# Strassen's seven block products for the FFNs' down projections, placed between the steps of the next group

## The chip, the cores and the metric

The kernel runs on one core of a Trainium2 chip. The metric is the device time of one execution in microseconds (us), the median of several. The core's engines are TensorE (PE in the profile: matrix multiplication; PEld is its weight load), VectorE (DVE), ScalarE (ACT), GpSimd (POOL) and SyncE (SP), which here issues the DMAs. Each works through its own queue in order; semaphores tie them together.

## What is computed

Two layers of a diffusion backbone: 512 latent tokens and 256 context tokens of width 1024. Each layer has four attention mixers and a feed-forward network (FFN) with a depthwise convolution over the tokens; layer 1 needs the latent tokens alone. What the change touches is the FFN:

```
def conv_ffn(h, w_up, conv_w, conv_b, w_down):
    u = depthwise_conv(h @ w_up, conv_w, conv_b)
    a, v = u[..., :FFN_DIM], u[..., FFN_DIM:]
    return (jax.nn.silu(a) * v) @ w_down

x = x + mod[:, 5, None] * rms_norm(f, g_ffn_post[l])
```

FFN_DIM is 2816, so w_up is 1024 x 5632 and w_down is 2816 x 1024. All is float32.

## The kernel before

Float32 products are made from halves. split (L249 on ACT, L255 on DVE or POOL) copies a value to a rounded "hi" in the type fp32r and takes the rest as "lo"; a product is then three matmuls, hi hi, hi lo and lo hi (mm3 at L268 to L270, token_mm at L1132). On POOL, split works in steps of 256 columns. Weights come by a DMA on SP (L260, 512 KB each) into the tile wr and are split into wh and wl.

The FFN is ffn_main, once a layer. FFN_DIM is cut into 22 blocks of 128. For a block there are two "ups" (the a half and the v half): 8 x 3 matmuls of 512 latent tokens and, in layer 0, 8 x 3 of 258 columns for the context, into a PSUM tile "up" (two of them). Each is followed by the convolution: ACT at L1226, DVE at L1227 and L1229, into the tile ut. Behind both stand Silu (ACT, L1233), the multiplication (DVE, L1234), the split of the result into gh and gl (POOL), and the load and split of the block's 1024 columns of w_down.

Blocks are taken in groups of [3, 3, 4, 4, 4, 4]. Behind a group, each token tile (128 tokens: six in layer 0, four in layer 1) gets its down projection from the group's blocks: per block three passes of two 512-column matmuls, six in all, with the tokens stationary, into a PSUM tile "dn" (two of them). It is copied to the accumulator of that tile by ACT (first group, L1267) or added by DVE (L1269). Behind the last group, post_norm normalises each token tile (Square on ACT at L550, a reciprocal square root in nine small DVE steps at L287 to L297, DVE at L587, the residual at L588 on POOL, on DVE for the last tile) and the tile is stored.

In layer 0, three steps of mod_steps stand at the end of each block: they multiply rows of the modulation weights (DMA into the tile wm, six buffers) by the conditioning vector on DVE (L502), once for each of one or two vectors.

The program doesn't run in the order in which it is written. The framework orders every engine's queue beforehand along a modelled time, by readiness and then by program order, and that order is then fixed; so a group's down matmuls stand in part between the ups of the same group and in part between those of the next.

## Time and profile before

| | us |
|---|---|
| median of 3 executions | 1946.42 |
| lowest and highest | 1942.38, 1950.67 |
| the profiled execution | 1949.91 |
| its span, first to last instruction | 1947.8 |
| mean granted clock of TensorE | 0.962 of full speed |

The span has layer 0's mixers up to about 540 us, its FFN to about 1120, layer 1's mixers to about 1475, its output projection to about 1575, and its FFN to the end. Times in rows are microseconds from the span's start unless marked ns. A row of a timeline gives start, length, engine, line, operation, out<-in and a count, and in brackets the idle time before it with what ended it. The end of a matmul is modelled, and matmuls overlap: a difference of starts is what one occupies.

### The profile page before, as it was taken

How to read it: one execution, taken by the hardware profiler on the slowest of the kernel's cores; microseconds unless marked ns; L12 is line 12 of the kernel's file. 1: busy time of each engine (PE TensorE's matmuls, PEld its weight loads, DVE VectorE, ACT ScalarE, POOL GpSimd, SP SyncE). 2: the span in 40 equal slices, each digit the busy share in tenths (PEclk: the TensorE clock that was granted, in tenths of full speed). 3: DMA queues.
4: the chain of work that ended last, by engine and by line, in shares of the span. 5: the costliest groups of instructions: out<-in, count | busy, mean ns of one | idle time of the engine just before them, and what ended most of it. 6: DMA issues, size and time to landing. Idle time of an engine off the chain costs nothing.

```text
span 1947.8 us, 27218 instructions
## 1 busy us (share of the span) xinstructions
PE 1809.6 (93%) x9834; PEld 1534.7 (79%) x9834; DVE 1085.1 (56%) x2119; ACT 905.4 (46%) x1597; POOL 995.0 (51%) x1216
## 2 busy tenths in 40 slices
PE   6999999898988999999999978979899899999997
PEld 3878788776887878888888867768787788888885
DVE  5456777775769545354322665775875622333335
ACT  4546557885542323131323454654886444333332
POOL 1464544544258547263625445753555265656653
PEclk7999899999998999999999999989999879999999
DMA  8663352644355324241312136524253322323322
GB/s 317 174 195 120 111 175 88 177 111 153 110 186 182 113 93 174 82 178 70 126 33 92 61 128 149 146 74 107 83 156 109 109 90 93 99 87 97 109 87 86
DMA packets 76166, 240.02 MB, mean 123 GB/s; under 512 B 11136, under 2 KB 12672, under 8 KB 73216
## 3 DMA queue, kind: packets, MB, share of 16 engines
q1 hardware_dynamic: 76032, 238.28, 38.8%
q8 instruction: 78, 1.28, 0.3%
q14 instruction: 56, 0.46, 0.1%
HBM read 201.94 MB, written 36.31 MB: 122 GB/s over the span
## 4 chain that ended last, share of the span: by engine, by line
PE 54%; DVE 7%; ACT 3%; issue 2%; POOL 2%; DMA 1%; SPq 0%; ACTq 0%; POOLq 0%; DVEq 0%
PE dn L1132 14%; PE up L268 9%; PE up L270 9%; PE up L269 9%; PE s L825 2%; PE wo L1132 2%; PE po L901 1%; PE tp L894 1%; DVE rs_w L293 1%; PE pj L268 1%; PE pj L269 1%; PE pj L270 1%; DVE rs_y L297 1%; DVE ptl L255 1%; DVE acc L587 1%
## 5 line engine op out<-in xcount | busy, mean ns | idle before, releaser
L255 POOL TENSOR_TENSOR wl<-wr,wh 128x256 fp32r<-128x256 f32 x706 | 568.4, 840 | 399.2 <-ACT wh L249 379.3
L249 ACT ACTIVATE wh<-wr 128x1024 fp32r<-128x1024 f32 (+1 forms) x186 | 193.6, 1050 | 401.6 <-PE up L269 202.7
L1227 DVE SCALAR_TENSOR_TENSOR ut<-up,pc,ut 128x769 f32<-128x769 f32 (+1 forms) x84 | 74.1, 883 | 347.5 <-ACT ut L1226 343.6
L268 PE MATMUL up<-hx,wh 128*128 128x512 f32 x672 | 263.2, 392 | 0.0
L269 PE MATMUL up<-hx,wh 128*128 128x512 f32 x672 | 262.6, 391 | 0.0
L270 PE MATMUL up<-hx,wl 128*128 128x512 f32 x672 | 262.4, 391 | 0.0
L825 PE MATMUL s<-op 128*128 128x256 f32 (+4 forms) x648 | 156.9, 351 | 21.4 <-ACT P L842 12.2
L255 DVE TENSOR_TENSOR ptl<-tp,pth 128x512 fp32r<-128x512 f32 (+1 forms) x208 | 136.1, 663 | 37.0 <-ACT pth L249 35.6
L870 POOL TENSOR_SCALAR P<-P,st 128x768 f32<-128x768 f32 (+2 forms) x120 | 96.7, 807 | 105.6 <-DVE st L846 70.4
L270 PEld LDWEIGHTS up<-hx,wl 128*128 128x128 f32 x672 | 126.5, 188 | 27.3
L268 PEld LDWEIGHTS up<-hx,wh 128*128 128x128 f32 x672 | 126.6, 188 | 25.5
L269 PEld LDWEIGHTS up<-hx,wh 128*128 128x128 f32 x672 | 126.6, 188 | 25.2
L1132 PE MATMUL dn<-wh,gh 128*128 128x512 f32 x440 | 140.4, 400 | 5.4 <-ACT gh L249 5.4
L1132 PE MATMUL dn<-wh,gl 128*128 128x512 f32 x440 | 137.5, 400 | 5.3 <-POOL gl L255 5.3
L825 PEld LDWEIGHTS s<-op 128*128 128x128 f32 (+1 forms) x648 | 108.7, 194 | 42.4 <-ACT P L842 20.7
L1132 PE MATMUL dn<-wl,gh 128*128 128x512 f32 x440 | 140.3, 398 | 0.0
L894 PE MATMUL tp<-ident,P 128*128 128x128 f32 x800 | 128.3, 282 | 10.0 <-DVE ptl L255 4.6
L255 POOL TENSOR_TENSOR gl<-ut,gh 128x256 fp32r<-128x256 f32 (+1 forms) x132 | 91.7, 722 | 75.9 <-ACT gh L249 74.1
L249 ACT ACTIVATE pth<-tp 128x512 fp32r<-128x512 f32 (+1 forms) x208 | 116.9, 577 | 29.1 <-PE tp L894 27.9
L842 ACT ACTIVATE P<-s,st 128x768 f32<-128x768 f32 (+2 forms) x120 | 94.3, 787 | 62.4 <-DVE st L833 25.2
L901 PE MATMUL po<-ptl,vt 128*128 128x256 f32 x400 | 112.4, 303 | 10.5 <-DVE ptl L255 9.8
L901 PE MATMUL po<-pth,vt 128*128 128x256 f32 x400 | 115.2, 304 | 7.0 <-ACT y L906 5.7
(286 smaller groups left out, 4315.3 us busy)
## 6 DMA issues: line engine op xcount, KB each, us to landing
wr<-wup SPq DMA_DIRECT2D x88, 512.0 KB, 3.7
wm<-wmod SPq DMA_DIRECT2D x56, 512.0 KB, 5.6
wr<-wdn SPq DMA_DIRECT2D x44, 512.0 KB, 3.8
op<-sc SPq DMA_DIRECT2D x36, 384.0 KB, 5.4
wr<-win SPq DMA_DIRECT2D x26, 512.0 KB, 4.2
wk<-wmk SPq DMA_DIRECT2D x12, 1024.0 KB, 7.5
op<-sc SPq DMA_DIRECT2D x60, 192.0 KB, 5.2
wm<-wm SPq DMA_DIRECT2D x8, 1024.0 KB, 9.4
```

The source lines that it names most:

```text
L249: self.nc.scalar.activation(out=hi, in_=src, func=AF.Copy)
L255: eng.tensor_tensor(out=d, in0=a, in1=b.bitcast(F32), op=ALU.subtract)
L268: mm(ps, lh, rh, start=first, stop=False)
L269: mm(ps, lh, rl, start=False, stop=False)
L270: mm(ps, ll, rh, start=False, stop=last)
L825: nc.tensor.matmul(full[:, o:o + w], q[:rows, qcol:qcol + P], k[:rows, c0:c0 + w], start=i == 0, stop=i == len(passes) - 1 and not msk)
L842: nc.scalar.activation(out=pt[:, :nk], in_=ps[:, :nk], func=AF.Exp, bias=nm, scale=scale, accum_out=rs)
L870: nc.gpsimd.tensor_scalar(out=a[:, :nk], in0=a[:, :nk], scalar1=ra, scalar2=1.0, op0=ALU.mult, op1=ALU.mult)
L894: nc.tensor.transpose(tp[:, a * 256 + j * P:a * 256 + (j + 1) * P], ptile[j][:, pos[kt]:pos[kt] + P], self.ident)
L901: nc.tensor.matmul(po[:, :256], vw, t[:, a * 256:(a + 1) * 256], start=n == 0, stop=n == total - 1)
L1132: mm(ps[:, c], a, b[:, c], start=first and i == 0, stop=last and i == 2)
L1227: nc.vector.scalar_tensor_tensor(out=u[:, 1:W], in0=ps[:, 0:W - 1], scalar=self.pcc(l, "w0", m), in1=u[:, 1:W], op0=ALU.mult, op1=ALU.add)
```

## The change

The down projection of every group but the last is made as a product of 2 x 2 blocks with Strassen's seven products instead of eight. A pair of blocks gives the two halves of the inner dimension (g1, g2 and w1, w2), even and odd token tiles give the two halves of the tokens, and the two 512-column halves of w_down those of the result. ntp is the number of token tiles in a half: three in layer 0, two in layer 1.

- operand(j) makes the two operands of product j for a pair: for products 3, 5, 6, 7 a sum or difference S of activations on DVE, for 4, 5, 6, 7 a difference T of weights (POOL in layer 0, DVE in layer 1), then the split of both: activations on ACT and DVE, weights on ACT and POOL (DVE for even j in layer 1). Each half has four buffers.
- product(j) makes the operands of all pairs of the group, runs their matmuls (mm3, 512 columns, tokens stationary) into the "dn" PSUM tiles and copies (first group, ACT) or adds (DVE) the result to one of seven accumulators in SBUF.
- The seven products of a group are put in a list, in the order 1, 2, 5, 6, 3, 4, 7, and called between the ups of the next group: two behind the first up of a block and one behind the second; four and three in the last group and in a group of two blocks.
- combine adds the seven accumulators up to the four blocks of the result: seven DVE additions over half of the tokens' columns each, once a layer, before the last group's additions.
- The last group is made as before, its matmuls in the order of mm3.
- Groups are [4, 4, 4, 4, 2, 4] in layer 0 and [4, 4, 4, 4, 4, 2] in layer 1.
- The raw blocks of w_down stay in SBUF (dr, four buffers, loaded once the previous group's products are done), the activations too (gr, six buffers); wm has two buffers instead of six, ut three instead of four in layer 0.

```diff
--- before
+++ after
@@ rms, post_norm, pre_norm @@
...
-        nc.vector.scalar_tensor_tensor(out=dst, in0=y, scalar=rs, in1=cg, op0=ALU.mult, op1=ALU.mult)
-        eng.tensor_tensor(out=dst, in0=dst, in1=x, op=ALU.add)
+        nc.vector.scalar_tensor_tensor(out=dst, in0=y, scalar=rs, in1=like(cg, y), op0=ALU.mult, op1=ALU.mult)
+        eng.tensor_tensor(out=dst, in0=dst, in1=like(x, dst), op=ALU.add)
...
@@ ffn_main and its new helpers @@
+    PLACE = dict(zip((1, 3, 4, 7, 2, 5, 6), range(7)))
+
+    def operand(self, j, pair, tmp, fp, ntp):
+
+        nc = self.nc
+        (g1, g2), (w1, w2) = pair
+        a11, a21, a12, a22 = (g.rearrange("p (t h c) -> p t h c", h=2, c=P)[:, :, x] for g in (g1, g2) for x in range(2))
+        b11, b12, b21, b22 = (w[:, 512 * x:512 * x + 512] for w in (w1, w2) for x in range(2))
+        if j in (5, 7):
+            tmp["s"] = fp.tile([P, ntp, P], F32, tag="S", bufs=2, name="S")
+            tmp["t"] = fp.tile([P, 512], F32, tag="T", bufs=2, name="T")
+        s, t = tmp.get("s"), tmp.get("t")
+
+        def s_(x, y, op):
+            nc.vector.tensor_tensor(out=s, in0=x, in1=y, op=op)
+
+        def t_(x, y):
+            (nc.gpsimd if ntp > 2 else nc.vector).tensor_tensor(out=t, in0=x, in1=y, op=ALU.subtract)
+
+        if j == 5:
+            s_(a21, a22, ALU.add)
+            t_(b12, b11)
+        elif j == 6:
+            s_(s, a11, ALU.subtract)
+            t_(b22, t)
+        elif j == 3:
+            s_(a12, s, ALU.subtract)
+        elif j == 4:
+            t_(t, b21)
+        elif j == 7:
+            s_(a11, a21, ALU.subtract)
+            t_(b22, b12)
+        x = {1: a11, 2: a12, 4: a22}.get(j, s)
+        w = {1: b11, 2: b21, 3: b22}.get(j, t)
+        ah, al = (fp.tile([P, ntp, P], F32R, tag=n, bufs=4, name=n) for n in ("ah", "al"))
+        bh, bl = (fp.tile([P, 512], F32R, tag=n, bufs=4, name=n) for n in ("bh", "bl"))
+        self.split(x, ah, al, nc.vector)
+        self.split(w, bh, bl, nc.gpsimd if ntp > 2 or j % 2 else nc.vector)
+        return ah, al, bh, bl
+
+    def product(self, j, pairs, tmps, fp, ntp, acc, first):
+
+        nc = self.nc
+        ops = [self.operand(j, p, t, fp, ntp) for p, t in zip(pairs, tmps)]
+        for t0 in range(0, ntp, 2):
+            n = min(2, ntp - t0)
+            ps = self.wide("dn", "dn")
+            for x in range(n):
+                t = t0 + x
+                for i, (ah, al, bh, bl) in enumerate(ops):
+                    self.mm3(ps[:, 512 * x:512 * x + 512], ah[:, t], al[:, t], bh, bl, i == 0, i == len(ops) - 1)
+            y = acc[:, self.PLACE[j], 512 * t0:512 * (t0 + n)]
+            if first:
+                nc.scalar.activation(out=y, in_=ps[:, :512 * n], func=AF.Copy)
+            else:
+                nc.vector.tensor_tensor(out=y, in0=y, in1=ps[:, :512 * n], op=ALU.add)
+
+    def inner(self, l, i, fp):
+
+        raw = fp.tile([P, 1024], F32, tag="dr", bufs=4, name="dr")
+        self.gate = self.nc.sync.dma_start(out=raw, in_=self.I["wdn"][l, i])
+        return raw
+
+    def combine(self, acc):
+
+        v = {j: acc[:, p] for j, p in self.PLACE.items()}
+        for out, x, y, op in ((6, 6, 1, ALU.add), (1, 1, 2, ALU.add), (7, 7, 6, ALU.add), (3, 3, 6, ALU.add), (3, 3, 5, ALU.add),
+                              (4, 7, 4, ALU.subtract), (7, 7, 5, ALU.add)):
+            self.nc.vector.tensor_tensor(out=v[out], in0=v[x], in1=v[y], op=op)
+
     def ffn_main(self, l, tiles, fp, h, early):
         nc, I = self.nc, self.I
         last = l == L - 1
         W = S if last else T + GAP
-        acc = {t: fp.tile([P, D], F32, tag="x", bufs=6, name="acc") for t in tiles}
-        sizes = [3, 3, 4, 4, 4, 4]
+        N = S if last else T
+        ntp = N // 256
+        acc = fp.tile([P, 7, ntp * 512], F32, name="acc")
+        sizes = [4, 4, 4, 4, 4, 2] if last else [4, 4, 4, 4, 2, 4]
         i = 0
         todo = None
         pend = []
+        work = []
...
         for gi, sz in enumerate(sizes):
             gt, dw = [], []
-            for i in range(i, i + sz):
+            fin = gi == len(sizes) - 1
+            for n, i in enumerate(range(i, i + sz)):
                 uv = []
                 for m in (i, NF + i):
                     if early:
@@ -1222,61 +1302,79 @@
...
-                    u = up.tile([P, T + GAP], F32, tag="ut", bufs=4, name="ut")
+                    u = up.tile([P, T + GAP], F32, tag="ut", bufs=4 if last else 3, name="ut")
...
                     uv.append(u)
+                    for _ in range((4, 3)[len(uv) - 1] if fin or sz == 2 else (2, 1)[len(uv) - 1]):
+                        if work:
+                            work.pop(0)()
                 a, v = uv
                 nc.scalar.activation(out=a[:, :W], in_=a[:, :W], func=AF.Silu)
-                nc.vector.tensor_tensor(out=a[:, :W], in0=a[:, :W], in1=v[:, :W], op=ALU.mult)
-                gh = fp.tile([P, T + GAP], F32R, tag="gh", bufs=5, name="gh")
-                gl = fp.tile([P, T + GAP], F32R, tag="gl", bufs=5, name="gl")
-                self.split(a[:, :W], gh[:, :W], gl[:, :W], nc.gpsimd)
-                gt.append((gh, gl))
-                dw.append(self.weights(I["wdn"][l, i], 1024, fp, ("dh", "dl"), 4))
+                g = fp.tile([P, N], F32, tag="gr", bufs=6, name="gr")
+                nc.vector.tensor_tensor(out=g[:, :S], in0=a[:, :S], in1=v[:, :S], op=ALU.mult)
+                if not last:
+                    nc.vector.tensor_tensor(out=g[:, S:], in0=a[:, S + GAP:W], in1=v[:, S + GAP:W], op=ALU.mult)
+                if fin:
+                    raw = self.wp.tile([P, 1024], F32, tag="wr", bufs=3, name="wr")
+                    self.gate = nc.sync.dma_start(out=raw, in_=I["wdn"][l, i])
+                    if n < 2:
+                        two = [[fp.tile([P, N], F32R, tag="gr", bufs=6, name="gp")] for _ in range(2)]
+                        dw.append([[fp.tile([P, 512], F32R, tag=y, bufs=4, name=y) for y in ("bh", "bl")] for _ in range(2)])
+                    else:
+                        two = [[fp.tile([P, ntp, P], F32R, tag=y, bufs=4, name=y).rearrange("p t c -> p (t c)") for _ in range(2)] for y in ("ah", "al")]
+                        d = [fp.tile([P, 1024], F32R, tag="dr", bufs=4, name="dp") for _ in range(2)]
+                        dw.append([[y[:, 512 * x:512 * x + 512] for y in d] for x in range(2)])
+                    c = N // len(two[0])
+                    for x, (gh, gl) in enumerate(zip(*two)):
+                        self.split(g[:, c * x:c * x + c], gh, gl, nc.gpsimd)
+                    for x in range(2):
+                        self.split(raw[:, 512 * x:512 * x + 512], *dw[-1][x], nc.gpsimd)
+                    gt.append([[y[t * P // c][:, t * P % c:t * P % c + P] for y in two] for t in range(N // P)])
+                else:
+                    gt.append(g)
+                    while not work and len(dw) < len(gt):
+                        dw.append(self.inner(l, i - n + len(dw), fp))
                 if l == 0:
                     with self.tc.issue_after(self.gate.ins):
                         if todo is None:
                             cb = self.cond(up)
                             order = [(0, 5, (0, 1)), (1, 1, (0, 1)), (1, 0, (0, 1))] + [(1, ch, (0,)) for ch in (2, 3, 4, 5)]
-                            todo = self.mod_steps(up, [(y, ch, f, vs) for y, ch, vs in order for f in range(KD)], cb, 6)
+                            todo = self.mod_steps(up, [(y, ch, f, vs) for y, ch, vs in order for f in range(KD)], cb, 2)
                         for _ in range(3):
                             todo()
             i += 1
-            fin = gi == len(sizes) - 1
...
+            if not fin:
+                pairs = [((gt[x], gt[x + 1]), (dw[x], dw[x + 1])) for x in range(0, sz, 2)]
+                tmps = [{} for _ in pairs]
+                work = [lambda j=j, p=pairs, t=tmps, f=gi == 0: self.product(j, p, t, fp, ntp, acc, f) for j in (1, 2, 5, 6, 3, 4, 7)]
+                continue
+            self.combine(acc)
...
             for t in tiles:
                 ps = self.wide("dn", "dn")
-                o = t * P + (GAP if t >= 4 else 0)
-                for k in range(sz):
-                    self.token_mm(ps, gt[k][0][:, o:o + P], gt[k][1][:, o:o + P], *dw[k], k == 0, k == sz - 1)
-                y = acc[t]
-                if gi == 0:
-                    nc.scalar.activation(out=y, in_=ps, func=AF.Copy)
-                else:
-                    nc.vector.tensor_tensor(out=y, in0=y, in1=ps, op=ALU.add)
-                if not fin:
-                    continue
+                for x in range(2):
+                    for k in range(sz):
+                        self.mm3(ps[:, 512 * x:512 * x + 512], *gt[k][t], *dw[k][x], k == 0, k == sz - 1)
+                y = acc[:, t % 2 * 2:t % 2 * 2 + 2, t // 2 * 512:t // 2 * 512 + 512]
+                nc.vector.tensor_tensor(out=y, in0=y, in1=like(ps, y), op=ALU.add)
...
```

## Rows read from the trace of the kernel before

**Rows 1.** The page: busy us, share of the span and instructions of each engine.
```profile
PE 1809.6 (93%) x9834; PEld 1534.7 (79%) x9834; DVE 1085.1 (56%) x2119; ACT 905.4 (46%) x1597; POOL 995.0 (51%) x1216
```

**Rows 2.** Windows: length, busy us and count of each engine, clock, DMA.
```profile
579.00:693.00 114.00, 104.13 (x520) 88.06 (x521) 87.64 (x115) 35.39 (x39) 85.79 (x75) 0.95 0.39 141
1578.00:1915.00 337.00, 337.00 (x1467) 276.22 (x1467) 105.14 (x121) 123.44 (x152) 206.38 (x290) 0.99 0.30 97
...
693.00:1082.00 389.00, 389.00 (x2056) 334.74 (x2056) 153.19 (x168) 103.46 (x110) 187.63 (x252) 1.00 0.31 106
```

**Rows 3.** Timeline of PE in layer 1's FFN: where runs of matmuls begin.
```profile
1733.71 0.64 PE L1132 MATMUL dn<-wh,gh 128*128 128x512 f32 x2
...
1744.86 0.39 PE L268 MATMUL up<-hx,wh 128*128 128x512 f32 x1
...
1755.74 0.63 PE L1132 MATMUL dn<-wh,gh 128*128 128x512 f32 x2
...
1799.69 0.63 PE L1132 MATMUL dn<-wh,gh 128*128 128x512 f32 x2
...
1865.68 0.63 PE L1132 MATMUL dn<-wh,gh 128*128 128x512 f32 x2
```

**Rows 4.** Timeline of PE in layer 0's FFN: a wait, and two group starts.
```profile
603.52 0.80 PE L1132 MATMUL dn<-wh,gh 128*128 128x512 f32 x1 [3.84 <-ACT gh L249]
...
800.36 0.63 PE L1132 MATMUL dn<-wh,gh 128*128 128x512 f32 x2
...
900.81 0.62 PE L1132 MATMUL dn<-wh,gh 128*128 128x512 f32 x2
```

**Rows 5.** Instructions of tiles and lines: count, ns min/median/max, first and last start.
```profile
L255 POOL TENSOR_TENSOR wl<-wr,wh x706: 719/742/1800, 30.7 to 1904.6; 128x256 fp32r<-128x256 f32 x177
...
L255 POOL TENSOR_TENSOR hx<-m,hx x4: 1273/1285/1300, 1130.5 to 1150.2; 128x512 fp32r<-128x512 f32 x4
...
L1269 DVE TENSOR_TENSOR acc<-acc,dn x50: 1205/1220/1223, 704.5 to 1937.4; 128x1024 f32<-128x1024 f32 x50
...
L588 DVE TENSOR_TENSOR acc<-acc,xr x2: 1225/1225/1225, 1135.3 to 1943.1; 128x1024 f32<-128x1024 f32 x2
...
L1227 DVE SCALAR_TENSOR_TENSOR ut<-up,pc,ut x39: 749/750/751, 1587.2 to 1898.5; 128x511 f32<-128x511 f32 x39
...
L1227 DVE SCALAR_TENSOR_TENSOR ut<-up,pc,ut x32: 1006/1018/1022, 611.0 to 1001.8; 128x769 f32<-128x769 f32 x32
...
L1234 DVE TENSOR_TENSOR ut<-ut x20: 702/1132/1349, 1582.9 to 1891.2; 128x512 f32<-128x512 f32 x20
...
L1234 DVE TENSOR_TENSOR ut<-ut x16: 950/961/1482, 618.5 to 986.7; 128x770 f32<-128x770 f32 x16
...
L502 DVE SCALAR_TENSOR_TENSOR wm<-wm,cb x56: 1209/1514/1760, 564.9 to 945.3; 128x1024 f32<-128x1024 f32 x56
...
L249 ACT ACTIVATE gh<-ut x20: 631/632/636, 1584.2 to 1892.5; 128x512 fp32r<-128x512 f32 x20
```

**Rows 6.** Timeline of POOL and DVE: steps beside another engine's long ones.
```profile
664.25 11.53 POOL L255 TENSOR_TENSOR wl<-wr,wh 128x256 fp32r<-128x256 f32 x8 [1.34 <-ACT wh L249]
...
1927.35 2.32 DVE L297 SCALAR_TENSOR_TENSOR rs_y<-rs_w,rs_y 128x1 f32<-128x1 f32 x1
...
1929.96 0.16 DVE L297 SCALAR_TENSOR_TENSOR rs_y<-rs_w,rs_y 128x1 f32<-128x1 f32 x1
```

**Rows 7.** The chain that ended last, at layer 1's end: start, us, what.
```profile
1887.94 2.32 PE dn L1132 x10
1901.16 2.79 PE dn L1132 x12
...
1914.62 0.24 PE up L270
...
1921.36 1.23 DVE acc L1269
```

**Rows 8.** DMA issues of layer 0's FFN: count, KB each, median us to landing.
```profile
wm<-wmod SPq DMA_DIRECT2D x56, 512.0 KB, 5.6
```

More of the change, by code (lines that the diff above doesn't have):

```diff
@@ L219, with like @@
          "l0 l1 l2 l3")
+def like(a, b):
+    return a.rearrange("p (a d) -> p a d", a=2) if len(b.shape) == 3 else a
 class Hidden:
@@ L546, in rms @@
     def rms(self, src, pool):
-        junk = pool.tile([P, D], mybir.dt.bfloat16, tag="sj", bufs=1, name="sj")
+        junk = like(pool.tile([P, D], mybir.dt.bfloat16, tag="sj", bufs=1, name="sj"), src)
         ss = self.sp.tile([P, 1], F32, tag="ss", bufs=4, name="ss")
@@ L593, in pre_norm @@
         xn = pool.tile([P, D], F32, tag="dgs", bufs=1, name="xn")
-        self.nc.scalar.activation(out=xn, in_=x, func=AF.Copy, scale=rs)
+        self.nc.scalar.activation(out=like(xn, x), in_=x, func=AF.Copy, scale=rs)
         return lambda: self.by_feature(xn, t, coef, h, pool)
@@ L1248, in ffn_main @@
             i += 1
-            fin = gi == len(sizes) - 1
-            if fin:
-                su.close()
-                self.psum(su, f"psU{l}", tr=4)
-                up = su.enter_context(self.tc.tile_pool(name=f"fin{l}", bufs=1, reuse_waits="tile"))
-                cg = {}
-                for t in tiles:
-                    self.gates(l, "ffn", t, cg, up, 2)
-                if not last:
-                    hn = Hidden(self.hp)
-                    coef = self.coefs(l + 1, "mix", tiles)
+            if not fin:
[3 more added lines that the diff above has]
+                continue
@@ L1260, in ffn_main @@
+            self.combine(acc)
+            su.close()
+            self.psum(su, f"psU{l}", tr=4)
+            up = su.enter_context(self.tc.tile_pool(name=f"fin{l}", bufs=1, reuse_waits="tile"))
+            cg = {}
+            for t in tiles:
+                self.gates(l, "ffn", t, cg, up, 2)
+            if not last:
+                hn = Hidden(self.hp)
+                coef = self.coefs(l + 1, "mix", tiles)
             for t in tiles:
                 ps = self.wide("dn", "dn")
-                o = t * P + (GAP if t >= 4 else 0)
@@ L1272, in ffn_main @@
+                y = acc[:, t % 2 * 2:t % 2 * 2 + 2, t // 2 * 512:t // 2 * 512 + 512]
+                nc.vector.tensor_tensor(out=y, in0=y, in1=like(ps, y), op=ALU.add)
                 self.post_norm(y, cg[t >= 4], self.xs[t], y, up, nc.vector if t == tiles[-1] else nc.gpsimd)
-                if f"xf{l}" in self.dump:
-                    nc.gpsimd.dma_start(out=self.dump[f"xf{l}"][t * P:(t + 1) * P], in_=y)
                 if last:
-                    nc.sync.dma_start(out=self.out[t], in_=y)
+                    nc.sync.dma_start(out=like(self.out[t], y), in_=y)
@@ L1277, in ffn_main @@
                     continue
                 if t < 4:
-                    nc.sync.dma_start(out=self.xs[t], in_=y)
+                    nc.sync.dma_start(out=like(self.xs[t], y), in_=y)
                 for f in pend:
```

## The prediction

> **What bounds the kernel now.** I read the busy times first, then the feed-forward stretches by windows, then TensorE's order of time inside them, then the durations of single operations, and last the order of time at the end. TensorE (PE) is busy for 93% of the span [rows 1]. In layer 0's FFN from 693 to 1082 us it is busy for 389.00 of 389 us, in layer 1's from 1578 to 1915 for all 337.00 [rows 2]: no other engine sets the pace there, and a matmul taken away is worth what it occupies. The reader should take that price from start to start, not from the duration that a row shows, since matmuls are pipelined: 48 down matmuls run from 1733.71 to 1744.86, 0.2323 us each, and the 48 up matmuls behind them end at 1755.74, 0.2267 us each [rows 3]. Four blocks take 65.99 us in layer 1 [rows 3] and 100.45 us in layer 0 [rows 4]; without the 96 and 144 down matmuls an up is (65.99 - 22.3) / 8 = 5.46 us, and (100.45 - 33.45) / 8 = 8.38 us. Before 693 us PE loses 114.00 - 104.13 = 9.9 us [rows 2], nearly all in four waits for down operands, the longest 3.84 us [rows 4].
>
> **Matmuls removed.** Multiplied out as before, two blocks cost 72 matmuls in layer 0 (six token tiles) and 48 in layer 1. The seven products cost 7 x 3 x 3 = 63 and 7 x 2 x 3 = 42. Nine pairs go that way in layer 0 (18 blocks) and ten in layer 1 (20 blocks): 81 and 60 fewer. In layer 0 the last group has four blocks as before, so all 81 come off ahead of the end: 81 x 0.2323 = 18.8 us. In layer 1 they don't. The stage ends with a chain: the last up ends at 1914.86, the first addition of a token tile to the accumulator starts at 1921.36 [rows 7], and the span ends at 1947.8, 32.9 us behind the last up. That tail is four tiles' normalisation. VectorE (DVE) spends on each an addition and a scaling of 1024 columns, 1.22 us each [rows 5], and nine steps like L297 of about 0.2 us [rows 6], some 4.3 us and ACT's squares between; PE's 24 matmuls take 5.6 us now. With 12 matmuls a tile the tail is DVE's, and at most 3 x 1.3, some 3 us, shorter. What counts is therefore what PE does before the last up ends. Before, five groups of 18 blocks (432 matmuls) and 10 + 12 of the last group [rows 7]; after, 420 and about 12. That is 22 x 0.2323 = 5.1 us, not 60 x 0.2323 = 13.9: the last group of two blocks moves work in front of the tail.
>
> The products accumulate three matmuls at a time in one bank, as the ups do, while a down matmul now changes banks every time. Their price lies between 0.2323 and 0.2267; nothing in the rows decides which, so I take half: 567 x 0.0028 = 1.6 us in layer 0, 1.2 us in layer 1.
>
> **Operands added.** Of each product, A is split by ACT and DVE, B by ACT and GpSimd (POOL), or by DVE for even products of layer 1; four products of a pair need a sum S (DVE), four a difference T (POOL in layer 0, DVE in layer 1). A two-input DVE operation takes 0.70 us on 512 columns at its least and 1.225 on 1024 [rows 5], so by a straight line 0.42 on 256 and 0.56 on 384. POOL takes 0.72 us at its least on 256 columns and 1.285 on 512, an eviction on DVE 1.22 on 1024 and about 0.75 (the 511-column row) on 512, ACT 0.63 us on 512 [rows 5].
>
> The products of a group stand in the first five ups of the next. Layer 1, PE: 5 x 5.46 + 84 x 0.2295 = 46.5 us. DVE: ten conv steps of 0.75 and two multiplications of 0.70, S 8 x 0.42, T 8 x 0.70, A 14 x 0.42, B 6 x 0.70, evictions 7 x 1.22, in all 36.3 us, 38 of the operations with two SBUF inputs. Layer 0, PE: 5 x 8.38 + 126 x 0.2295 = 70.8. DVE: conv 10.2, multiplications 2.2, S and A 22 x 0.56, evictions 7 x 1.97, six L502 steps 7.7: 46. POOL: 5 x 4 x 0.72 = 14.4 for the up weights, 14 x 1.44 + 8 x 1.285 = 30.4 for the products: 45. ACT gets at most 28 x 0.63 = 17.6 us in a group and loses the splits of four blocks; it was busy 123 of 337 us [rows 2] and stays off the path.
>
> **The price that decides.** A two-input DVE operation waits for a POOL instruction. Seen in rows: the 128x1 step L297, 0.16 us by itself, took 2.32 beside POOL's 1024-column addition, and POOL's 256-column subtractions stretched from 0.72 to 11.53 / 8 = 1.44 us where L502 ran [rows 6]. Each engine works in order: behind a DVE operation that waits stand the evictions that free the two down buffers in PSUM and the conv steps that free the ups', and PE waits for both. How long the new operations wait no row shows; three that wait today have medians 0.01 us (L1234, layer 0), 0.31 (L502) and 0.43 (L1234, layer 1) above their least [rows 5]. I take their mean, 0.25, and keep 0.01 and 0.43 as ends. The Trainium skill says in "SBUF — State Buffer", Who interferes with whom, that such an instruction and a GpSimd instruction that reads SBUF exclude each other for the whole instruction; these rows agree nearly. By that rule layer 1's burst would fill the shared interface: 20.5 us of DVE and 36 x 0.72 = 25.9 us of POOL in 46.5, which is the second rival below.
>
> With 0.25, layer 1's burst costs DVE 36.3 + 38 x 0.25 = 45.8 us against PE's 46.5. Buffers for two products let DVE start about 3 us ahead. So nothing piles up, yet nothing is to spare: I charge 1 us for each of four groups where PE's order, fixed beforehand, meets an operand that is late, +4 (0 to 10). Layer 0 has 54 against 70.8; only the two-block group, with seven products between two ups (45.7 us of PE, 42 of DVE, 36 of POOL before its own waits), is tight. The first group now has no down matmuls, so the waits of before 693 us go but for one; in their place I put one wait like them (2.5 us) in most groups with products, two where L502 still runs twice a step, 13 us in all (3 to 25): +3.1 against the 9.9 of before.
>
> **Other moves.** combine puts 7 additions (8.6 us) on DVE. In layer 0 six ups hide them. In layer 1 they lie between the last product and the first tile's addition; from the last group's start PE needs 4 x 5.46 + 19.2 = 41 us to the last up's end, and the addition can come 6.5 us later, as now: 47.5. DVE needs conv 6.0, multiplications 1.4, products 27.4 and combine 8.6 = 43.4, with 45 waits of 0.25 54.7; less the 3 us of lead the tail slips by 4.2 (-3 to +12). The wmod loads have two buffers instead of six: on the SP queue a load now waits for the L502 two steps back, and the next up weights are queued behind it. Landing is 5.6 us [rows 8], so two links of load and L502 are 2 x (5.6 + 1.5) = 14.2 us, under the 16.8 us of a block's two ups: nothing, while that cover holds. The raw down loads wait for the previous group's last product, with three ups to spare.
>
> **Sum.** -18.8 - 1.6 + 3.1 in layer 0; -5.1 - 1.2 + 4 + 4.2 in layer 1: -15.4 us. The profiled execution took 1949.9 us (span 1947.8), 3.5 over the median of 1946.4; from its 1949.9 I come to 1934.5, and in terms of the median to 1931 us.
>
> **Rivals.**
> - All is covered. No operand is late, products run at 0.2267: -18.8 - 3.2 - 9.9 - 5.1 - 2.4 - 3 = -42, 1904 us. For it: in layer 1 POOL has less to do than before (per group 16 product splits of 0.72 us in place of 24 of weights and activations); against: PE waited four times before in a lighter stage.
> - Operands become the bound, slower than before. If a two-input DVE operation waits 0.43 us, layer 1's burst takes 36.3 + 16.3 = 52.6, 3.1 more than PE and the lead, in three groups (in the first products ACT evicts) +9, with 4 as above +13; the tail slips 12; layer 0's waits come to 25, +15, and the products keep 0.2323: -18.8 + 15 - 5.1 + 13 + 12 = +16, 1962 us. It decides from (46.5 + 3 - 36.3) / 38 = 0.35 us of waiting on. For it: L1234 waits 0.43 in this very stretch; against: L502's 0.31 under heavier traffic.
> - The SP queue holds up weights. With landings over 6.9 us the wmod chain outlasts a block of layer 0's first group; four blocks at 3 us are +12: 1943 us.
> - PE doesn't give back what it saves, because the order fills the freed slots badly (no row speaks to this): no change, 1946 us.
>
> **Chances.** Forecast 0.45 (own range 1920 to 1942), all covered 0.20, operands 0.20, SP 0.10, no change 0.05. A measurement tells about 0.5% (9.7 us) from no change. Faster: 0.32 of the forecast's and the 0.20, 0.52; slower: 0.17 of the operands', 0.03 of SP's and 0.02 of worse, 0.22; within: 0.26. The range takes in both outer cases nearly: 1905 to 1960.
>
> **What would show it.** Right: PE at full busy share through 693 to 1060 us, four blocks in about 96 us in layer 0 and 63 in layer 1, seven products at 0.227 to 0.232 us a matmul, waits of PE on DVE's or POOL's operand writes of a us or two, and in layer 1 a last up some 5 us earlier but a tail longer than 33 us. Wrong: PE idle by several us a group in layer 1, or medians of the 128x256 DVE subtractions above 0.42 + 0.35 us (the operands' rival); PE waiting for up weights behind a wmod load (SP); a tail that shrinks with its matmuls (my reading of the end).

## The result, and the profile after

The changed kernel takes 1928.28 us (median of 4 runs, 1922.15 to 1929.78), the kernel before 1948.55 beside it (4 runs, 1942.38 to 1952.0): a ratio of 0.9895, interval 0.9867 to 0.9923, 20 us or 1.05% faster. The forecast was 1931 us and faster. The profiled execution of after took 1928.22 us, with a span of 1926.4; that of before 1949.9 and 1947.8. The rest of this section takes the 21.4 us between the spans apart.

First the page of after, busy time of each engine, and the chain that ended last by engine.

```profile
PE 1769.0 (92%) x9693; PEld 1503.6 (78%) x9693; DVE 1334.1 (69%) x2478; ACT 972.5 (50%) x1806; POOL 1058.8 (55%) x1192
...
PE 49%; DVE 11%; ACT 3%; DMA 2%; issue 2%; POOL 2%; SPq 0%; ACTq 0%; DVEq 0%; POOLq 0%
```

Against [rows 1]: 141 matmuls fewer (81 + 60, as counted), 40.6 us less of TensorE, and 249 us more of VectorE. Nearly twice as much of TensorE's time went as of the program's (40.6 against 21.4 us), so some of it came back as waits. To see where, the same stretches as in [rows 2], each cut at the last up of its layer (length, busy us and count of PE, PEld, DVE, ACT, POOL, clock, DMA share, GB/s).

```profile
579.00:693.00 114.00, 102.46 (x536) 87.10 (x535) 99.61 (x131) 41.56 (x60) 83.03 (x71) 0.99 0.44 149
693.00:1062.00 369.00, 365.52 (x1950) 316.76 (x1949) 253.54 (x314) 129.95 (x187) 254.71 (x272) 1.00 0.34 113
1560.00:1886.00 326.00, 326.00 (x1430) 269.78 (x1430) 231.36 (x314) 155.02 (x253) 201.06 (x249) 0.99 0.29 96
1886.00:1926.40 40.40, 15.95 (x54) 10.77 (x52) 27.47 (x52) 7.30 (x13) 13.62 (x10) 0.75 0.22 78
```

Layer 0 idles for 11.5 us before 693 us and 3.5 behind it, and then no more before the last up; layer 1 does not idle at all up to its last up; the last row is the tail, in which PE is busy for 16 of 40 us. A layer's stretch is now measured from the start of its first up to the end of its last. In layer 0 that is 561.43 to 1081.27 us before and 561.54 to 1062.71 after; two windows of each kernel, cut at 693, add up to it (sum lines, before and then after):

```profile
sum 519.84, PE 509.34 PEld 436.89 DVE 257.42 ACT 147.05 POOL 286.37; mean PE 254.67 PEld 218.45 DVE 128.71 ACT 73.53 POOL 143.18
```

```profile
sum 501.17, PE 486.15 PEld 419.88 DVE 369.01 ACT 182.79 POOL 354.70; mean PE 243.07 PEld 209.94 DVE 184.51 ACT 91.40 POOL 177.35
```

So layer 0 gained 18.7 us: PE has 23.2 us less to do and idles 4.5 us more. What lies between the two FFNs took 497.03 and 497.45 us. Layer 1's stretch went from 336.5 us (1578.30 to 1914.84) to 326.1 (1560.16 to 1886.25), 10.4 less; the tail from 33.0 to 40.15, 7.2 more. Sum: -18.7 + 0.4 - 10.4 + 7.2, and 0.1 ahead of it, make the -21.4.

Three readings of after explain these sizes. **The price.** In the timeline of PE, 24 down matmuls begin at the first row and the next up at the second:

```profile
1619.53 0.39 PE L273 MATMUL dn<-bh,ah 128*128 128x512 f32 x1
...
1624.97 0.39 PE L273 MATMUL up<-hx,wh 128*128 128x512 f32 x1
```

That is 5.44 / 24 = 0.2267 us each, the price of the ups, where before paid 0.2323 [rows 3]. **Layer 0's waits** (timeline of PE, those over 0.75 us up to the last up):

```profile
603.17 0.36 PE L273 MATMUL up<-hc,wh 128*128 128x258 f32 x1 [2.54 <-DVE ut L1309]
613.34 0.36 PE L273 MATMUL up<-hc,wh 128*128 128x258 f32 x1 [1.59 <-DVE ut L1309]
635.96 0.50 PE L273 MATMUL dn<-bh,ah 128*128 128x512 f32 x1 [0.90 <-ACT ah L254]
641.84 0.50 PE L275 MATMUL dn<-bh,al 128*128 128x512 f32 x1 [3.75 <-DVE al L260]
```

Two more, of 1.16 and 2.32 us behind DVE's L1309, come at 707 and 718. All lie in the first two groups and in the first products, where a modulation step runs L507 (before: L502) twice on VectorE; in the chain from 579 to 693 us L507 and its loads make 46%. The two-block group, which the prediction called tight, shows no wait. **The tail** (timelines of DVE, POOL and PE from the last up's end at 1886.25):

```profile
1886.64 1.44 DVE L1275 TENSOR_TENSOR acc<-acc 128x1024 f32<-128x1024 f32 x1
1888.00 0.74 DVE L1307 SCALAR_TENSOR_TENSOR ut<-up,pc,ut 128x511 f32<-128x511 f32 x1
1888.66 1.76 DVE L1275 TENSOR_TENSOR acc<-acc 128x1024 f32<-128x1024 f32 x1
1890.34 0.74 DVE L1309 SCALAR_TENSOR_TENSOR ut<-up,pc,ut 128x511 f32<-128x511 f32 x1
1891.00 1.21 DVE L1275 TENSOR_TENSOR acc<-acc 128x1024 f32<-128x1024 f32 x1
1892.13 0.68 DVE L1318 TENSOR_TENSOR gr<-ut 128x512 f32<-128x512 f32 x1
1900.84 1.22 DVE L1371 TENSOR_TENSOR acc<-acc,dn 128x1024 f32<-128x1024 f32 x1 [8.03 <-PE dn L275]
```

```profile
1892.95 1.90 POOL L567 TENSOR_TENSOR dgs<-ident,gate 128x1024 f32<-128x1024 f32 x1 [3.62 <-DVE gr L1318]
1894.81 1.41 POOL L260 TENSOR_TENSOR gp<-gr,gp 128x256 fp32r<-128x256 f32 x2
```

```profile
1893.53 0.79 PE L273 MATMUL dn<-bh,gp 128*128 128x512 f32 x1 [5.91 <-ACT gp L254]
...
1895.40 3.61 PE L572 MATMUL tr<-dgs,ones 128*128 128x512 f32 x4
```

The combination's additions (L1275) stand between the conv steps of the last up on VectorE, so that the last block's multiplication ends 6.6 us after the last up; before, its end was 3.2 us after it. Behind it POOL makes the gate's diagonal (dgs) ahead of the split that PE waits for, where before it came behind that split. PE, idle for 5.91 us, then makes the transposes in 3.61 us (1.98 before): from 1892.5 to 1899.2 us its granted clock is 0.50, the lower of the two levels (1.2 GHz), where before it was 1.00 from the last up to 1939.9. The first addition comes 14.6 us after the last up, where it was 6.5 [rows 7]; 0.9 us is given back after it.

### The profile page after: what moved, and what is told of

Read it like the earlier page. It is cut to its first block, busy times and chain, and to the rows that moved or that the text cites. A ratio compares the mean times of both kernels' runs of the same rounds, so it can differ in the third digit from the quotient of the medians.

```text
span 1926.4 us, 27715 instructions
## 1 busy us (share of the span) xinstructions
PE 1769.0 (92%) x9693; PEld 1503.6 (78%) x9693; DVE 1334.1 (69%) x2478; ACT 972.5 (50%) x1806; POOL 1058.8 (55%) x1192
## 4 chain that ended last, share of the span: by engine, by line
PE 49%; DVE 11%; ACT 3%; DMA 2%; issue 2%; POOL 2%; SPq 0%; ACTq 0%; DVEq 0%; POOLq 0%
PE up L273 9%; PE up L274 9%; PE up L275 8%; PE dn L275 4%; PE dn L273 4%; PE dn L274 4%; PE s L830 2%; PE wo L1137 2%; PE po L906 1%; PE tp L899 1%; DVE wm L507 1%; DVE junk L507 1%; DMA wm<-wmod 1%; DVE rs_w L298 1%; DMA op<-sc 1%
## 5 line engine op out<-in xcount | busy, mean ns | idle before, releaser
L260 POOL TENSOR_TENSOR wl<-wr,wh 128x256 fp32r<-128x256 f32 x530 | 443.7, 868 | 320.2 <-ACT wh L254 304.2
L254 ACT ACTIVATE wh<-wr 128x1024 fp32r<-128x1024 f32 (+1 forms) x142 | 148.5, 1048 | 248.1 <-PE up L274 125.3
L899 PE MATMUL tp<-ident,P 128*128 128x128 f32 x800 | 126.9, 280 | 10.4 <-DVE ptl L260 4.7
L275 PE MATMUL dn<-bh,al 128*128 128x512 f32 x329 | 128.5, 391 | 3.7 <-DVE al L260 3.7
L273 PE MATMUL dn<-bh,ah 128*128 128x512 f32 x329 | 128.3, 390 | 0.9 <-ACT ah L254 0.9
L274 PE MATMUL dn<-bl,ah 128*128 128x512 f32 x329 | 128.3, 390 | 0.0
L260 POOL TENSOR_TENSOR bl<-T,bh 128x256 fp32r<-128x256 f32 x112 | 104.4, 958 | 42.1 <-ACT bh L254 42.1
L838 DVE TENSOR_REDUCE st<-s 128x1 f32<-128x768 f32 (+2 forms) x120 | 95.3, 807 | 39.9 <-PE s L830 39.6
```

Of the source, the lines that this page charges most:

```text
L254: self.nc.scalar.activation(out=hi, in_=src, func=AF.Copy)
L260: eng.tensor_tensor(out=d, in0=a, in1=b.bitcast(F32), op=ALU.subtract)
L273: mm(ps, lh, rh, start=first, stop=False)
L274: mm(ps, lh, rl, start=False, stop=False)
L275: mm(ps, ll, rh, start=False, stop=last)
L838: nc.vector.tensor_reduce(out=nm, in_=ps[:, :nk], axis=AX.X, op=ALU.max, negate=True)
```

## The experiments

Each time is the median of a kernel; behind "beside" stands that of the kernel before in the same session. Each ratio is to that kernel, and the range in brackets is its 95% interval.

**The order of the matmuls alone.** The kernel before, its down matmuls half by half with three in a row in one bank, as the ups.

```diff
+ for c in (slice(0, 512), slice(512, 1024)):
+     for k in range(sz):
+         self.mm3(ps[:, c], gt..., dw[k][0][:, c], dw[k][1][:, c], k == 0, k == sz - 1)
- for k in range(sz):
-     self.token_mm(ps, ...)
```

> The kernel before with one edit: a token tile's down matmuls go through one 512-column half after the other, three matmuls at a time as in the ups, instead of changing the half with every matmul. Theory 1 (the price of a matmul falls from 0.2323 to 0.2267 us by this order alone): 792 matmuls in layer 0 and 454 ahead of the last up in layer 1 save 1246 x 0.0056 = 7 us, about 1941 us, and the products' lower price is no merit of Strassen's. Theory 2 (the lower price comes from the operands' new tiles): no change, 1948 us.

1949.66 us beside 1947.33; ratio 1.002 (1.0003 to 1.0036). In its timeline of PE 48 down matmuls begin at the first row, the next up at the second: 0.2317 us each.

```profile
1732.87 0.40 PE L268 MATMUL dn<-wh,gh 128*128 128x512 f32 x1
...
1743.99 0.39 PE L269 MATMUL up<-hx,wh 128*128 128x512 f32 x1
```

The order brings 0.0006 of the 0.0056 us. The reason that the prediction offered for a lower price falls. The order isn't free, though. It puts ten of the last group's matmuls behind the last up, and there PE waits for the last block's split, 2.50 us where before it waited 0.63:

```profile
1916.24 0.78 PE L268 MATMUL dn<-wh,gh 128*128 128x512 f32 x1 [2.50 <-ACT gh L249]
```

The first addition comes 9.7 us after the last up (6.5), and the tail is 37.8 us long (33.0). The changed kernel's last group has this order too.

**The width of the activations' tiles.** The kernel before, with gh and gl in tiles of 896 columns in place of 770; nothing more is computed.

```diff
- gh = fp.tile([P, T + GAP], F32R, tag="gh", bufs=5, name="gh")
+ gh = fp.tile([P, 896], F32R, tag="gh", bufs=5, name="gh")
... (gl the same)
```

> The kernel before with the tiles of the split activations (gh, gl) 896 columns wide instead of 770, nothing else; the added columns are never used. Theory 1 (the down matmul's 0.2323 us against the product's 0.2267 comes from where the 770-column tiles lie): the price falls to 0.2267, 1246 x 0.0056 = -7 us, about 1940 us. Theory 2 (it has another cause): 1947 us.

1938.07 us beside 1947.36; ratio 0.9945 (0.9924 to 0.9967). 48 down matmuls in its timeline:

```profile
1785.13 0.62 PE L1132 MATMUL dn<-wh,gh 128*128 128x512 f32 x2
...
1796.01 0.39 PE L268 MATMUL up<-hx,wh 128*128 128x512 f32 x1
```

10.88 / 48 = 0.2267: the old order has the new price as soon as the tile is wider. It is the activation tile's layout that costs, and the changed kernel, whose products take their activations from tiles of 384 and 256 columns (128 a token tile), gets rid of it by the way. Its size: from the first to the last up, layer 0 fell by 3.1 us and layer 1 by 2.7 in this profile, 5.8 together. The 9 us of the medians are more than that; the profile has the rest ahead of layer 0's FFN (-3.1) and between the FFNs (-6.8), where no down matmul runs, at a mean clock of 0.970 (0.962 before). The stretch between the FFNs, which no experiment touches, took 495.2 to 503.1 us in the profiles of all other kernels here, and 490.2 in this one. That part isn't explained. By the ratios (0.9945 and 0.9895) the changed kernel is some 10 us ahead of this one, where it is 20 ahead of the kernel before.

**The same with 784 columns**, so that a row begins at a multiple of 64 bytes.

```diff
- gh = fp.tile([P, T + GAP], F32R, tag="gh", bufs=5, name="gh")
+ gh = fp.tile([P, 784], F32R, tag="gh", bufs=5, name="gh")
... (gl the same)
```

> The kernel before, with the split activations (gh, gl) in tiles of 784 columns where it had 770, so that a row is 3136 bytes long (a multiple of 64) where it was 3080 (only a multiple of 8); the tile with 896 columns (3584 bytes) gave 0.2267 us a down matmul in place of 0.2323. Theory 1 (the place at which the rows, and so the stationary 128 columns, begin): 784 does as much as 896, 48 down matmuls take 10.9 us, and the kernel is 9 to 10 us faster than before, about 1937. Theory 2 (something else that the larger tiles shift, such as a stretch of SBUF that the 896-column tiles no longer share with others): 784 columns keep 0.2323, 48 down matmuls take 11.15 us, and the time stays within 3 us of the kernel before.

1946.33 us beside 1945.31; ratio 0.9996 (0.9971 to 1.0021). Timeline of PE, 48 down matmuls, 11.11 / 48 = 0.2315 us each:

```profile
1735.70 0.40 PE L1132 MATMUL dn<-wh,gh 128*128 128x512 f32 x1
...
1746.81 0.40 PE L268 MATMUL up<-hx,wh 128*128 128x512 f32 x1
```

A multiple of 64 bytes is not what counts. The trace after adds two more widths: the last groups' first two blocks have their activations in tiles of 768 columns (layer 0) and 512 (layer 1), and their matmuls occupy 0.227 us too (median of the differences of starts). So the widths with the low price (256, 384, 512, 768, 896) are multiples of 128 columns or 512 bytes, and the two with the high one (770, 784) are not. Whether that is the cause, or the place at which a tile lies, no run separates.

**The groups alone.** The kernel before with the new groups.

```diff
- sizes = [3, 3, 4, 4, 4, 4]
+ sizes = [4, 4, 4, 4, 4, 2] if last else [4, 4, 4, 4, 2, 4]
```

> The kernel before with the changed kernel's group sizes alone, all down projections multiplied out. Theory 1 (in layer 1 what counts is the matmuls ahead of the last up, and a last group of two blocks moves 26 to 31 there): +6 to +7 us, less up to 3 for the shorter tail, 1951 to 1955 us. Theory 2 (the larger first groups remove the 9.9 us of early waits, and the gain of the change is largely theirs): 1938 to 1940 us.

1946.3 us; ratio 0.9994 (0.9978 to 1.001). Its parts move and cancel: layer 0's stretch 514.2 us (-5.6), layer 1's 342.1 (+5.6), the tail 31.3 (-1.7). Of the two theories each has its part: the first is right for layer 1 and the tail, the second for some of the early waits in layer 0 (PE's idle time there 6.9 us, before 10.5), not for the gain. It also gives a better starting point for the products. From here to the changed kernel layer 1's stretch falls by 342.1 - 326.1 = 16.0 us, and 60 matmuls of 0.2323 with 0.0056 on the 420 left are 13.9 + 2.4 = 16.3. Layer 0's falls by 13.0; 81 matmuls and 567 x 0.0056 are 22.0, and PE's idle time rises from 6.9 us to 15.0, which leaves 13.9.

**A matmul's worth.** The changed kernel without product 7 (its place in combine is taken by product 6).

```diff
- ... for j in (1, 2, 5, 6, 3, 4, 7)]
+ ... for j in (1, 2, 5, 6, 3, 4)]
- ... (7, 7, 6, ALU.add) ...
+ ... (7, 6, 6, ALU.add) ...
```

> The changed kernel without product 7 (its operands, matmuls and accumulation left out, combine takes nothing for it), so the result lacks it. Theory 1 (PE sets the pace among the products, and a matmul is worth its 0.2267 us): 9 x 9 + 10 x 6 = 141 matmuls less, -32 us, about 1896 us. Theory 2 (the operands on DVE and POOL set the pace): a seventh of the products' DVE work goes too, some 4 us per group where DVE is the bound; the gain then differs from 32 by several us, above all in layer 1, where PE would show idle time that shrinks.

1891.38 us; ratio 0.9712 (0.9671 to 0.9753), 37 us under the changed kernel by the medians and 36 by the ratios. From first to last up layer 0 took 18.0 us less and layer 1 14.6; 81 and 60 matmuls of 0.2267 are 18.4 and 13.6. So a matmul is worth its price in both layers, to within 1 us, and the operands of a product have room beside it. The 4 us over the expected 32 lie outside the two stretches.

**Longer GpSimd instructions.** The changed kernel, with POOL's splits in the main part of the FFN in one instruction of up to 1024 columns where they were cut into 256.

```diff
- step = 256 if eng is self.nc.gpsimd and len(src.shape) == 2 else n
+ step = (1024 if self.one else 256) if eng is self.nc.gpsimd and len(src.shape) == 2 else n
... (self.one is set from the start of ffn_main to combine)
```

> The changed kernel with POOL's subtractions of the FFNs in one instruction each (up to 1024 columns, some 2.4 us) instead of steps of 256; the work is the same. Theory 1 (a two-input DVE operation waits for POOL's running instruction, and from a mean wait of 0.35 us on layer 1's products make DVE the bound): the mean wait, 0.20 us as run, goes to 0.5 to 0.9, layer 1 loses 6 us and more in each of three groups, layer 0 about as much, +20 to +45 us, 1948 to 1973. Theory 2 (the waits are hidden whatever their length): 1928 or a little less, since POOL saves the fixed part of three instructions in four.

1924.94 us; ratio 0.9875 (0.9845 to 0.9906), not slower. DVE's two-input operations in layer 1, 1600 to 1880 us (line, operation, out<-in, shapes, count, busy us, mean ns), of the changed kernel:

```profile
L260 DVE TENSOR_TENSOR al<-S,ah 128x256 fp32r<-128x256 f32 x40 | 24.8, 622 | 0.0
L1318 DVE TENSOR_TENSOR gr<-ut 128x512 f32<-128x512 f32 x18 | 19.2, 1066 | 0.3
L260 DVE TENSOR_TENSOR al<-gr,ah 128x256 fp32r<-128x256 f32 x27 | 18.7, 704 | 2.1 <-ACT ah L254 1.9
L1221 DVE TENSOR_TENSOR S<-gr 128x256 f32<-128x256 f32 x19 | 16.4, 876 | 0.3
```

and with longer POOL instructions:

```profile
L262 DVE TENSOR_TENSOR al<-S,ah 128x256 fp32r<-128x256 f32 x38 | 27.0, 711 | 0.0
L1223 DVE TENSOR_TENSOR S<-gr 128x256 f32<-128x256 f32 x18 | 18.3, 1014 | 0.3
L262 DVE TENSOR_TENSOR al<-gr,ah 128x256 fp32r<-128x256 f32 x26 | 17.7, 694 | 2.1 <-ACT ah L256 1.9
L1321 DVE TENSOR_TENSOR gr<-ut 128x512 f32<-128x512 f32 x17 | 12.6, 741 | 0.3
```

Over all groups of such operations in that view, 190 took 138.6 us in the changed kernel; with the prediction's 0.42 us for 256 columns (106 of them) and 0.70 for 512 (84) that is a mean wait of 35.3 / 190 = 0.19. With the longer instructions 183 took 142.0, 0.23. Single waits grow, the mean hardly does: one POOL instruction of 1024 columns takes 2.43 us where four of 256 took 4 x 0.80, so there is less POOL time to meet (145.1 us in this stretch in place of 173.4). The longest S<-gr took 2.54 us here, 0.96 in the changed kernel. The Trainium skill's rule in "SBUF — State Buffer", Who interferes with whom (the one engine waits out the other's whole instruction) is not contradicted by these rows. What the prediction's rival made of the waits, that they hold TensorE up, did not come: it is busy for 280.00 of these 280 us in the changed kernel and for 279.57 with the longer instructions.

**More on VectorE.** The changed kernel, all B splits of layer 1's products on DVE.

```diff
- self.split(w, bh, bl, nc.gpsimd if ntp > 2 or j % 2 else nc.vector)
+ self.split(w, bh, bl, nc.gpsimd if ntp > 2 else nc.vector)
```

> The changed kernel, with the subtraction of every B split of layer 1's products on VectorE, where the odd products' were on GpSimd. That moves 8 subtractions of 512 columns in a group of four blocks. By the prediction's sum, with the mean wait of 0.20 us that the trace after shows, VectorE's work in a group of layer 1 goes from 36.3 + 38 x 0.20 = 43.9 us to 36.3 + 8 x 0.70 + 46 x 0.20 = 51.1, against 46.5 of TensorE and 3 of lead. Theory 1 (the point from which VectorE is the bound is as reckoned): TensorE idles in layer 1, some 1.6 us in each of four groups, 6 in all, and the combination before the tail comes later by 3 to 6; together 5 to 12 us slower than the changed kernel, 1933 to 1940. Theory 2 (there is more room than the sum says, since GpSimd has less to do and so holds VectorE up less): TensorE stays at full busy share from 1600 to 1880 us, and the time is within 3 us of the changed kernel's.

1927.18 us; ratio 0.9918 (0.9891 to 0.9944): no difference to the changed kernel that the intervals resolve. Layer 1's stretch took 325.3 us, the tail 40.0. Windows 1600 to 1880 us of the changed kernel and of this one, and DVE's rows of this one:

```profile
1600.00:1880.00 280.00, 280.00 (x1237) 231.82 (x1236) 208.85 (x287) 135.59 (x226) 173.38 (x214) 1.00 0.30 98
```

```profile
1600.00:1880.00 280.00, 280.00 (x1237) 231.99 (x1236) 205.31 (x324) 138.13 (x228) 115.81 (x142) 1.00 0.30 98
```

```profile
L260 DVE TENSOR_TENSOR al<-S,ah 128x256 fp32r<-128x256 f32 x40 | 18.6, 466 | 1.6 <-ACT ah L254 1.6
L260 DVE TENSOR_TENSOR al<-gr,ah 128x256 fp32r<-128x256 f32 x27 | 12.7, 482 | 2.0 <-ACT ah L254 1.9
L1221 DVE TENSOR_TENSOR S<-gr 128x256 f32<-128x256 f32 x19 | 8.5, 448 | 0.2
```

DVE ran 37 instructions more and was busy 3.5 us less, while POOL was busy 57.6 us less. 226 two-input operations took 138.6 us, by the same reckoning 0.045 us of wait each. The exchange is cheap: a subtraction of 512 columns holds DVE for 0.68 us at the least, and POOL for two times 0.73. The second theory holds: a wait is no constant of the operation, it goes with what POOL has to do at the time.

**The modulation steps later.** Fewer of them in layer 0's first blocks, three at a time from the ninth block on.

```diff
- for _ in range(3):
+ for _ in range((1, 2, 2, 2, 2, 2, 2, 2)[i] if i < 8 else 3):
      todo()
```

> The changed kernel with fewer modulation steps (L507) behind layer 0's first eight blocks, one and then two each instead of three, the rest later. Theory 1 (these steps and their two-buffered loads are what PE waits for ahead of 740 us, some 15 us of idle in all): PE's waits there halve, -7 us, about 1921 us. Theory 2 (the products' operands and their waits for POOL are what PE waits for): the waits stay, 1928 us.

1932.29 us; ratio 0.9922 (0.9898 to 0.9945), an interval that overlaps the change's own. The waits at 636, 642, 707 and 718 us are gone, those at 603 and 613 stay, and others come later, among them these at the end of the layer (timeline of PE; the last up ends at 1065.8):

```profile
1036.43 0.36 PE L273 MATMUL up<-hc,wh 128*128 128x258 f32 x1 [1.61 <-DVE ut L1309]
...
1071.50 0.80 PE L273 MATMUL dn<-dp,ah 128*128 128x512 f32 x1 [3.92 <-ACT ah L254]
```

Layer 0's stretch took 503.4 us (501.2), PE's idle time in it 16.0 (15.0). Neither theory holds as it stands: the waits neither halve nor stay, they move with the steps. The steps cost where they stand beside products, early or late.

**The combination left out** in layer 1 (the seven accumulators stay as they are).

```diff
- self.combine(acc)
+ if not last:
+     self.combine(acc)
```

> The changed kernel without combine's seven additions in layer 1 (the blocks of the result are then the plain accumulators). Theory 1 (five of the seven run behind the last product and hold up the last conv steps): the last up's conv ends 3 us earlier and the tail falls from 40.3 to about 37 us. Theory 2 (the gates' work on POOL and PE sets the tail's start): the tail stays within 1 us of 40.

This is one execution. Tail 36.1 us (1890.59 to 1926.7) in place of 40.15, PE's wait in it 2.47 us in place of 5.91:

```profile
1894.42 0.50 PE L273 MATMUL dn<-bh,gp 128*128 128x512 f32 x1 [2.47 <-ACT gp L254]
```

Three other kernels here with the changed kernel's tail (no_seven, b_on_dve, mods_later) have 39.8 to 40.2 us for it, so the combination costs 4 us of the tail. The whole time was 1928.49 us, with 5.4 us more between the FFNs than the changed kernel had, so that the span says nothing.

**Four blocks at the end.** The changed kernel, with the last group of layer 1 as in layer 0.

```diff
- sizes = [4, 4, 4, 4, 4, 2] if last else [4, 4, 4, 4, 2, 4]
+ sizes = [4, 4, 4, 4, 2, 4]
```

> The changed kernel with layer 1's groups as layer 0's, [4, 4, 4, 4, 2, 4], so that its last group has four blocks. Theory 1 (combine and the products' additions crowd DVE just behind the last up, and a last group of two leaves them nowhere to go): 20 to 42 matmuls fewer ahead of the last up, -5 to -9 us, and the tail goes back from 40 to about 33 us, -7: 1912 to 1916 us against 1928. Theory 2 (the tail is long by the gates and the order of the end itself): only -5 to -9, about 1921 us; theory 3 (what is taken from the products comes back as matmuls in the tail): 1928.

1922.5 us; ratio 0.9882 (0.9859 to 0.9905), which overlaps the change's interval. Layer 1's stretch fell to 320.9 us, and the tail stayed at 40.5, as the second theory has it. The combination is done early here; now 84 matmuls of the last group and the gates' transposes lie in the tail, and DVE waits for them:

```profile
1889.34 1.22 DVE L1371 TENSOR_TENSOR acc<-acc,dn 128x1024 f32<-128x1024 f32 x1 [8.75 <-PE dn L275]
```

**The gates' rows early.** The gates of layer 1 made in the first block of the last group, in a bank of the down projections, with the groups of the change (gates_early) and with four blocks at the end (four_gates).

```diff
+ if last and fin and n == 0:
+     self.gates(l, "ffn", 0, cg, fp, 1, lambda: self.wide("cgp", "dn")[:, :512])
...
```

> The changed kernel with layer 1's gate rows (POOL's 1.9 us dgs, two matmuls, two copies) made in the last group's first block instead of behind the last up. Theory 1 (they hold up the lo half of the last block and put 3.3 us of PE's transposes between its down matmuls): the first addition comes 4 to 5 us earlier, 1923 to 1924 us against 1928. Theory 2 (DVE's combine sets the tail): no change.

> The changed kernel with both edits: layer 1's last group of four blocks, and its gate rows in that group's first block. Theory 1 (the two add up: -6 as measured, and -4 to -5): about 1917 us. Theory 2 (with four blocks in the tail PE has 74 down matmuls there, and moving the gates only shifts its wait): 1921 to 1922 us.

gates_early took 1926.54 us, ratio 0.9898 (0.9875 to 0.992), and four_gates 1921.21 us, ratio 0.9867 (0.9845 to 0.9889), the lowest median of the kernels that compute the whole result. In the traces the tails are 37.2 and 36.5 us, 3 and 4 less than without; in the times that is less than the intervals resolve. By its time gates_early lies between its theories, and four_gates where the second has it. The interval of four_gates also overlaps the change's own.

## Why the prediction came out right, and where its steps were off

**What bounds it** held: PE, at full share through both stretches but for layer 0's first waits, and no_seven confirms the price of a matmul.

**Layer 0**, -17.3 predicted (-18.8 - 1.6 + 3.1), -18.7 measured. The 81 matmuls are as counted. The price fell by the whole 0.0056 us, 3.2 us in place of 1.6. PE's idle time is 15.0 us for 13 put down; its place was half right. The waits lie beside L507, but the later groups, each of which was charged 2.5 us, have none. From 579 to 693 us the granted clock was 0.99 (0.95 before), which goes the same way as the 1.2 us by which PE's busy time fell beyond 18.8 + 3.2; no run was made on it.

**Layer 1 up to the last up**, -2.3 predicted (-5.1 - 1.2 + 4), -10.4 measured: the step that missed most. First, 12 matmuls of the last group were put ahead of the last up as a carry-over from [rows 7]; none is there. PE goes from 454 down matmuls to 420, 34 x 0.2323 = 7.9 us. Second, the price, 420 x 0.0056 = 2.4. Third, the +4 of stalls is nil. -7.9 - 2.4 = -10.3.

**The tail**, +4.2 predicted, +7.2 measured. The cause named, the combination on DVE, is worth 4 us by no_combine. The other 3 weren't in the sum. Two things can account for them: POOL's diagonal ahead of the last split with the transposes at the lower clock behind PE's idle time, which go with the gates (gates_early takes 3 us off the tail), and the last group's half-by-half order, which made the tail of the kernel before 4.8 us longer (order_alone). No run gives the changed kernel the old order back, so how the rest divides is open; against groups_alone, whose last group has two blocks as well, the tail is 8.9 us longer. The two misses, 8 us on one side and 3 on the other, leave 5 us of the 6 between the -15.4 forecast and the -21.4 of the spans. That the forecast lies so close is in part luck.

**The price's reason** was wrong. The prediction said that nothing in the rows decides, and offered the order of the banks; order_alone refutes that and gh_wide gives the tile. Without that run the change would look better than it is: in the two stretches 5.8 of the 21.4 us are had in the kernel before by one number, and by the medians 9 of the 20.

**The wait of 0.25 us** was sized well (0.19), and treated wrongly. As a constant it made a threshold of 0.35 from which the change loses. Since the waits fall with POOL's load, work shifted from POOL to DVE costs no time (b_on_dve), and the rival in which operands become the bound was given too much with 0.20. The sign named for it, medians of the 128x256 subtractions above 0.77 us, misleads: in the trace after al<-gr has 0.95 and S<-gr 0.85, al<-S 0.44, and TensorE still doesn't idle in that stretch. Two slips in the sums change nothing: a straight line through the rows gives 0.44 and 0.57 us for 256 and 384 columns, not 0.42 and 0.56, and the terms of VectorE's burst add up to 36.5, not 36.3. The rival in which all is covered was right for layer 1's stretch and wrong for layer 0's start and the tail. The wmod loads with two buffers landed in 3.8 us (5.6 in [rows 8]); with their steps they are on the chain from 579 to 693 us, but none of the long waits of PE there names a load: that rival did not occur. What the two buffers cost by way of VectorE no run shows, since none gives wm its six buffers back.

## What to carry to other kernels

Before an algebraic change is credited with its gain, take the price of the operation that it removes and of the one that it puts in from start to start, and try the side effects (tile widths, group sizes) alone. Where a kernel is bound by TensorE through a stretch, a matmul removed there is worth its price, and what is added on other engines was paid here mostly at the stretch's ends, where nothing covers it. A contention wait that was read at one load is not a constant of the operation.

## What the runs showed of the hardware that was not expected

- A 128x512 matmul with its stationary 128 columns from a tile 770 columns wide took 0.2323 us from start to start, from one of 784 columns 0.2315, from one of 896, 384 or 256 columns 0.2267, and from one of 768 or 512 columns 0.227 (median). Its weight loads show 188 ns in all of them. The cause is open.
- A POOL subtraction of 1024 columns took 2.43 us on the mean, one of 256 columns 0.80 in the same stretch.
- 36 two-input operations more on DVE cost it no busy time when they were taken from POOL: 138.6 us for 226 in place of 138.6 for 190.
